# Grouped attention on one core: one store per head, V cast into place, loads in order of need, VectorE chains of eight

## The chip, the cores and the metric

One Trainium2 chip, one of its cores. The metric is the device time of one execution in microseconds (us), from repeated executions. A profile of one execution gives every instruction with start and duration. The span of a profile is some 1.8 us shorter than the time of the same execution. Engines: PE is TensorE, PEld its weight loads, DVE is VectorE, ACT is ScalarE, POOL is GpSimd, SP is SyncE. "L427" is line 427 of the kernel that was profiled, so the same line of code has other numbers in other kernels.

## The reference

Eight batches, eight query heads, two K/V heads (four query heads share one), 1024 positions, head size 64, all fp32:

```python
scores = scale * np.matmul(q_group, k_group.transpose(0, 1, 3, 2))
attn = np.exp(scores - np.max(scores, axis=-1, keepdims=True))
attn = attn / (np.sum(attn, axis=-1, keepdims=True) + 1e-08)
output[:, q_start:q_end] = np.matmul(attn, v_group)
```

## The kernel before

The work is cut into 128 jobs (a job is one half of the queries of one head) of eight cells (128 keys x 512 queries). A cell is one score matmul into PSUM (the memory that its matmuls write; the kernel has two buffers of it for each use, below called banks), an exponential, and four output matmuls, whose 65th column sums the weights. Two engines compute exponentials: ScalarE takes pairs of cells with its own function, VectorE takes single cells and computes the bits of a bf16 exponential, then corrects them in a chain of four steps over `GROUP` cells at once.

```python
GROUP = 4
...
def exp_bits(cell, n, g, slot):          # first step, cell by cell, out of PSUM
    nc.vector.tensor_scalar(out=groups[g][:, slot], in0=psum.pop(cell),
        scalar1=bits_scale, scalar2=bits_bias, op0=ALU.mult, op1=ALU.add)
def exp_curve(g, m, step):               # the chain, over m cells
    step 0: z = pd & 0x7F                # tensor_scalar
    step 1: y = z * A/128 + B            # tensor_scalar
    step 2: y = z * y                    # tensor_tensor
    step 3: pd = pd + y                  # tensor_tensor
...
def normalise(s):                        # job done: divide, then store half a head
    nc.vector.reciprocal(out=rec, in_=o[:, :, D])
    nc.vector.tensor_tensor(out=ost, in0=o[:, :, 0:D], in1=rec..., op=ALU.mult)
    nc.sync.dma_start(out=out[b, h]...[side], in_=ost)
```

(The chain is abridged to a line per step.) `make_plan` simulates the engines with fixed costs when the kernel is built, and lays down the order of all instructions. A cell goes to whichever of the two engines has a free PSUM bank first, in the order of the cells. Q, K and V are cast to bf16 by GpSimd's DMA into a scratch tensor in memory, Q and K come back through transposing DMAs, V through two placements.

The softmax here doesn't subtract the row's maximum and nothing guards it: scores larger than these inputs give would overflow.

Of the kernel before, what the change touches and what calls it, by code (L numbers as in the profile page):

```python
# [14 lines left out]
GROUP = 4  # L15


def make_plan(nj, nkc):
# [6 lines left out]
    QK, PV, EXP, P1, NORM = 0.214, 0.143, 0.925, 0.605, 0.57  # L25
    CHAIN = (0.73, 0.73, 1.26, 1.26)
    FROM_PE, FROM_ACT, FROM_DVE = 0.28, 0.18, 0.12
    LIVE_A, LIVE_D, PENDING, ONLY_A = 26, 6, 8, 14
    INF = 1e9
    n = nj * nkc  # L30
# [3 lines left out]
    nxt = 0  # L34
# [7 lines left out]

    def first_free(slots):
        return min(range(len(slots)), key=lambda s: slots[s])

    while normed < nj:
        best = None
        if nxt < n:
            ta = td = INF
            if open_a is not None:  # L50
                ta = max(pe, open_a["t"])
            elif live["A"] < LIVE_A:
                ta = max(pe, min(a_free))
            if pending < PENDING and nxt < n - ONLY_A and (cur or live["D"] < LIVE_D):
                td = max(pe, min(bank))
            t, to_d = (ta, 0) if ta <= td else (td, 1)
            if t < INF:
                best = min(best or (INF,), (t, 1 + to_d, "qk", to_d))
        for i, s in enumerate(open_jobs):
            for c in rem[s]:  # L60
                at = max(pe, ready.get(s * nkc + c, INF))
                if at < INF:
                    best = min(best or (INF,), (at, 3 + i, "pv", (s, c)))
        if len(open_jobs) < 2 and next_job < nj:
            at = max(pe, min(obank_free), min(ready.get(next_job * nkc + c, INF) for c in range(nkc)))
            if at < INF:
                best = min(best or (INF,), (at, 3 + len(open_jobs), "open", next_job))
        for q, p, kind in ((normq, 0, "norm"), (p1q, 1, "p1"), (chainq, 2, "chain")):
            if q:
                best = min(best or (INF,), (max(dve, q[0][0]), p, kind, 0))  # L70
        if cur and nxt >= n - ONLY_A and not p1q:
            best = min(best or (INF,), (dve, 9, "flush", 0))
        t, _, kind, arg = best
        if kind == "qk":
            cell = nxt
            nxt += 1
            pe = t + QK
            if not arg:
                if open_a is None:
                    slot = first_free(a_free)  # L80
                    a_id += 1
                    live["A"] += 1
                    open_a = {"slot": slot, "t": a_free[slot], "cells": []}
                    a_free[slot] = INF
                o = open_a
                ops.append((t, "qk", cell, "A", a_id, o["slot"], len(o["cells"])))
                o["cells"].append(cell)
                home[cell] = ("A", a_id)
                if len(o["cells"]) == 2 or nxt >= n:
                    act = max(act, pe + FROM_PE)  # L90
                    ops.append((act, "exp", a_id, tuple(o["cells"])))
                    act += EXP * len(o["cells"]) / 2
                    a_free[o["slot"]] = act + FROM_ACT
                    uses[("A", a_id)] = len(o["cells"])
                    for x in o["cells"]:
                        ready[x] = act + FROM_ACT
                    open_a = None
            else:
                k = first_free(bank)
                bank[k] = INF  # L100
                pending += 1
                ops.append((t, "qk", cell, "D", k, 0, 0))
                p1q.append((pe + FROM_PE, cell, k))
# [41 lines left out]
        elif kind == "flush":  # L145
            chainq.append((dve, d_id, cur, 0))
            cur = []
        else:
            _, g, cells, step = chainq.pop(0)
            ops.append((t, "chain", g, len(cells), step))  # L150
            dve = t + CHAIN[step] * len(cells) / GROUP
            if step + 1 < len(CHAIN):
                chainq.insert(0, (dve, g, cells, step + 1))
            else:
                pending -= len(cells)
                uses[("D", g)] = len(cells)
                for x in cells:
                    ready[x] = dve + FROM_DVE
# [4 lines left out]
def kernel(  # L163
# [27 lines left out]
    PIECE = 256  # L191
    scale = 1.0 / math.sqrt(D)
# [15 lines left out]
    qT_pool = ctx.enter_context(tc.tile_pool(name="qTpool", bufs=8))  # L208
    kT_pool = ctx.enter_context(tc.tile_pool(name="kTpool", bufs=4))
    pa_pool = ctx.enter_context(tc.tile_pool(name="papool", bufs=26))  # L210
    pd_pool = ctx.enter_context(tc.tile_pool(name="pdpool", bufs=6))
    tmp_pool = ctx.enter_context(tc.tile_pool(name="tmppool", bufs=2))
    ostage_pool = ctx.enter_context(tc.tile_pool(name="ostage", bufs=10))
# [11 lines left out]

    ident = const_pool.tile([128, 128], BF16)
    make_identity(nc, ident)
    vsets, ksets = [], []
    for s in range(2):
# [4 lines left out]
        for side in range(2):  # L234
            if s == 0:
                nc.vector.memset(ks[(1 - side) * D : (2 - side) * D, :, side, :], 0.0)
        ksets.append(ks)

# [41 lines left out]
    def place_v(b, g):  # L280
        for two in range(2):
            nc.sync.dma_start(
                out=vsets[b % 2][:, g, two * NHC : (two + 1) * NHC, 0:D],
                in_=scratch[("v", b, g)].rearrange(
                    "(c p two d) -> two p c d", p=128, two=2, d=D
                )[two],
            )

    def first_loads():

        staged = []
        for eng, src in ((nc.sync, k[0, 0]), (nc.scalar, q[0, 0])):
            f = first_pool.tile([128, NHC, 2, D], FP32, name=f"f{len(staged)}")
            eng.dma_start(
                out=f, in_=src.rearrange("(c p two) d -> p c two d", p=128, two=2)
            )
            staged.append(f)
        vf = first_pool.tile([128, NHC, 2, D], FP32, name="vf")
        nc.sync.dma_start(
            out=vf, in_=v[0, 0].rearrange("(c p two) d -> p c two d", p=128, two=2)  # L300
        )
        cast(("q", 0, 1), q[0, 1])
        for two in range(2):
            nc.gpsimd.tensor_copy(
                out=vsets[0][:, 0, two * NHC : (two + 1) * NHC, 0:D],
                in_=vf[:, :, two, :],
            )
        for side in range(2):
            nc.gpsimd.memset(ksets[1][(1 - side) * D : (2 - side) * D, :, side, :], 0.0)  # L309
        fk, fq = staged  # L310

        hk = first_pool.tile([128, NHC, 3, D], BF16, name="hk")
        nc.vector.tensor_copy(out=hk[:, :, 0:2, :], in_=fk)  # L313
        nc.vector.tensor_copy(out=hk[:, :, 2, :], in_=fk[:, :, 0, :])
        hq = first_pool.tile([128, NHC, 2 * D], BF16, name="hq")
        nc.scalar.copy(out=hq, in_=fq.rearrange("p c two d -> p c (two d)"))
        tk = dbanks[0].tile([128, 2, HALF], BF16, name="dps0")
        tq = dbanks[1].tile([128, HALF], BF16, name="dps1")
        for w in range(2):
            for c in range(NHC):  # L320
# [5 lines left out]
        for c in range(NHC):  # L326
            nc.tensor.transpose(tq[:, c * 128 : (c + 1) * 128], hq[:, c, :], ident)
        qT[(0, 0)] = qT_pool.tile([128, HALF], BF16, name="qT")
        lo, hi = slice(0, D), slice(D, 2 * D)
        nc.vector.tensor_copy(out=ksets[0][lo, 0, 0, 0:HALF], in_=tk[lo, 0, :])  # L330
        nc.scalar.copy(out=qT[(0, 0)], in_=tq)
        nc.vector.tensor_copy(out=ksets[0][lo, 0, 0, HALF:S], in_=tk[lo, 1, :])
        nc.vector.tensor_copy(out=ksets[0][hi, 0, 1, 0:HALF], in_=tk[hi, 1, :])
        nc.vector.tensor_copy(out=ksets[0][hi, 0, 1, HALF:S], in_=tk[hi, 0, :])
# [4 lines left out]
    temps = {}  # L339
    ops_of = {}  # L340
# [82 lines left out]
    def normalise(s):  # L423
# [4 lines left out]
        ost = ostage_pool.tile([128, NQS, D], FP32, name="ost")  # L428
        nc.vector.tensor_tensor(  # L429
            out=ost,  # L430
# [3 lines left out]
        )  # L434
        nc.sync.dma_start(
            out=out[b, h].rearrange("(s p two) d -> two p s d", p=128, two=2)[side],
            in_=ost,
        )


    events = []

    def at(t, f, *args):
        events.append((t, len(events), f, args))
# [4 lines left out]
    for op in plan:  # L449
        if op[1] == "qk":  # L450
            first_use.setdefault(op[2] // NKC, op[0])
        at(op[0], run[op[1]], *op[2:])
    for b in range(B):
        for h in range(H):
            if b == 0 and h == 0:
                continue
            th = first_use[(b * H + h) * 2]
            if (b, h) != (0, 1):
                at(th - 28.0, cast, ("q", b, h), q[b, h])
            for n in range(HALF // PIECE):  # L460
                at(th - 17.0 + n, transpose_q, b, h, n)
            if h % HPG == 0:
                g = h // HPG
                at(th - 38.0, cast, ("k", b, g), k[b, g])
                at(th - 33.0, cast, ("v", b, g), v[b, g])
                for n in range(HALF // PIECE):
                    at(th - 27.0 + n, transpose_k, b, g, n)
                for side in range(2):
                    for parity in range(2):
                        at(th - 20.0, place_k, b, g, side, parity)  # L470
                at(th - 15.0, place_v, b, g)
# [34 lines left out]
```

## Time and profile before

| | us |
|---|---|
| time, median (4 runs) | 397.54 (397.33 to 398.27) |
| span of the profile | 395.6 |
| start of the first exponential on ScalarE | 8.16 |
| first exponential to the end of the last | 380.05 |
| from there to the end of the span (the tail) | 7.4 |

These three stretches are how the run is read below. In the middle ScalarE is hardly ever idle, so the middle can shrink only if it has fewer exponentials or none of them waits; start and tail are chains of single steps. The lines of this profile are in the prediction.

### The profile page before, as it was taken

To read this page: it belongs to the slowest core of one execution; us is meant where nothing else is said; L and a number is where in the kernel's file an instruction comes from. 1 tells how busy PE (TensorE), PEld (TensorE's weight loads), DVE (VectorE), ACT (ScalarE), POOL (GpSimd) and SP (SyncE) were. 2 spreads that over 40 slices of the span, in tenths; PEclk is the share of its full clock that TensorE was granted. 3 is DMA by queue.
4 is the path that set the end of the run, shared out by engine and by line. 5 is a ranking of instruction groups with operands and counts; after the bars stand their busy time and mean duration, and the time that the engine had idled before them with its cause. 6 is when DMAs were issued, how large, how long until landed. Compare 5 with 4: busy or idle time off the path is not lost.

```text
span 395.6 us, 12683 instructions
## 1 busy us (share of the span) xinstructions
PE 365.7 (92%) x5043; PEld 233.0 (59%) x5132; DVE 375.8 (95%) x664; ACT 381.5 (96%) x415; POOL 86.6 (22%) x165
## 2 busy tenths in 40 slices
PE   4899999999999999999999999999999999999986
PEld 2455566565656556655656565565655666565655
DVE  4999999999999999999999999999999999999995
ACT  4999999999999999999999999999999999999992
POOL 5340303132041313113131040312214131120000
PEclk9999999999999999999999999999999999999999
DMA  4665866749676786847758686785965867574314
GB/s 106 106 125 111 163 107 127 128 86 160 103 139 130 132 143 101 142 90 145 115 103 141 111 141 112 118 143 98 155 109 115 149 132 121 99 130 99 68 28 94
DMA packets 134890, 46.72 MB, mean 118 GB/s; under 512 B 130848, under 2 KB 132384, under 8 KB 133344
## 3 DMA queue, kind: packets, MB, share of 16 engines
q1 hardware_dynamic: 129408, 29.52, 38.3%
q0 software_dynamic: 4896, 16.13, 27.0%
q8 instruction: 40, 0.66, 0.8%
q10 hardware_dynamic: 528, 0.26, 0.2%
q14 instruction: 18, 0.15, 0.2%
HBM read 27.13 MB, written 28.97 MB: 142 GB/s over the span
## 4 chain that ended last, share of the span: by engine, by line
ACT 67%; DVE 11%; PE 10%; issue 6%; DMA 3%; POOL 1%; SPq 0%
ACT pa L362 67%; PE ops L414 5%; PE aps L351 5%; DVE pd L371 3%; DVE y L402 2%; DVE pd L406 2%; DVE ost L429 1%; DMA vf<-in_v_dram 1%; PE dps L351 1%; DVE y L392 1%; DMA qT<-scr_q 1%; POOL kset L309 1%; DVE z L386 1%; DVE rec L427 1%; DMA scr_q<-in_q_dram 1%
## 5 line engine op out<-in xcount | busy, mean ns | idle before, releaser
L362 ACT ACTIVATE pa<-aps 128x1024 bf16<-128x1024 f32 x412 | 379.0, 1064 | 2.1 <-PE aps L351 1.3
L351 PE MATMUL aps<-qT,kset 128*128 128x512 bf16 x735 | 226.2, 379 | 15.5 <-ACT pa L362 13.6
L414 PEld LDWEIGHTS <-pa 128*128 128x128 bf16 x3296 | 134.5, 97 | 57.6 <-DVE ost L429 0.8
L414 PE MATMUL ops<-vset,pa 128*128 128x65 bf16 x3296 | 143.9, 193 | 3.4
L371 DVE TENSOR_SCALAR pd<-dps 128x512 uint16<-128x512 f32 x200 | 129.8, 682 | 2.2 <-PE dps L351 2.2
L351 PEld LDWEIGHTS <-kset 128*128 128x128 bf16 x1024 | 85.3, 97 | 66.3 <-issue 30.9
L248 POOL DMA_DIRECT2D scr_q<-in_q_dram x63 | 34.0, 540 | 173.4 <-PE aps L351 150.6
L351 PE MATMUL dps<-qT,kset 128*128 128x512 bf16 x200 | 64.5, 380 | 1.0
L406 DVE TENSOR_TENSOR pd<-pd,y 128x2048 uint16<-128x2048 uint16 x50 | 61.2, 1225 | 1.7
L402 DVE TENSOR_TENSOR y<-z,y 128x2048 f16<-128x2048 uint16 x50 | 61.2, 1225 | 1.7
L429 DVE TENSOR_TENSOR ost<-ops,rec 128x256 f32<-128x256 f32 x128 | 54.3, 425 | 4.4
L414 PEld LDWEIGHTS <-pd 128*128 128x128 bf16 x800 | 38.5, 97 | 29.8 <-DVE pd L406 7.9
L268 POOL DMA_DIRECT2D kset<-kT x60 | 32.2, 545 | 76.7 <-DMA kT<-scr_k 68.7
L414 PE MATMUL ops<-vset,pd 128*128 128x65 bf16 x800 | 45.3, 194 | 1.2
L392 DVE TENSOR_SCALAR y<-z 128x2048 f16<-128x2048 uint16 x50 | 34.3, 687 | 0.6
L386 DVE TENSOR_SCALAR z<-pd 128x2048 uint16<-128x2048 uint16 x50 | 34.2, 684 | 0.0
L427 DVE RECIPROCAL rec<-ops 128x4 f32<-128x4 f32 x128 | 22.6, 176 | 2.4 <-PE ops L414 1.9
L248 POOL DMA_DIRECT2D scr_v<-in_v_dram x15 | 7.6, 505 | 8.2 <-PE aps L351 7.1
L248 POOL DMA_DIRECT2D scr_k<-in_k_dram x15 | 8.1, 542 | 4.7 <-PE aps L351 4.3
L321 PE MATMUL dps<-ident,hk 128*128 128x128 bf16 x8 | 1.0, 311 | 5.0 <-DVE hk L313 5.0
L321 PEld LDWEIGHTS <-hk 128*128 128x128 bf16 x8 | 0.8, 141 | 5.0 <-DVE hk L313 5.0
L309 POOL MEMSET kset<- 64x2048 bf16 x2 | 3.6, 1798 | 0.1
(20 smaller groups left out, 9.7 us busy)
## 6 DMA issues: line engine op xcount, KB each, us to landing
out_dram<-ost SPq DMA_DIRECT2D x128, 128.0 KB, 3.2
scr_q<-in_q_dram POOLq DMA_DIRECT2D x63, 128.0 KB, 3.5
kset<-kT POOLq DMA_DIRECT2D x60, 64.0 KB, 2.7
qT<-scr_q SPq DMA_TRANSPOSE x126, 3.6
scr_k<-in_k_dram POOLq DMA_DIRECT2D x15, 128.0 KB, 4.2
scr_v<-in_v_dram POOLq DMA_DIRECT2D x15, 128.0 KB, 3.9
vset<-scr_v SPq DMA_DIRECT2D x30, 64.0 KB, 3.8
kT<-scr_k SPq DMA_TRANSPOSE x30, 3.4
```

The lines of the kernel that those rows point to most:

```text
L248: dma = nc.gpsimd.dma_start(out=scr.rearrange("(p f) -> p f", f=1024), in_=src.rearrange("(p s) d -> p (s d)", s=1024 // D),)
L268: nc.gpsimd.dma_start(out=ksets[b % 2][side * D : (side + 1) * D, g, side, parity * HALF : (parity + 1) * HALF], in_=kT[(b, g)][parity * D ...
L351: last_score[0] = nc.tensor.matmul(dst, lhsT=ksets[b % 2][:, h // HPG, side, c * 128 : (c + 1) * 128], rhs=qT[(b, h)], start=True, stop=Tr ...
L362: nc.scalar.activation(out=pt[:, 0:m], in_=psum.pop(("A", n))[:, 0:m], func=AF.Exp, scale=scale)
L371: nc.vector.tensor_scalar(out=groups[g][:, slot], in0=psum.pop(cell), scalar1=bits_scale, scalar2=bits_bias, op0=ALU.mult, op1=ALU.add,)
L386: nc.vector.tensor_scalar(out=z, in0=pd, scalar1=0x7F, scalar2=None, op0=ALU.bitwise_and)
L392: nc.vector.tensor_scalar(out=y, in0=temps[g][0], scalar1=CURVE_A / 128.0, scalar2=CURVE_B, op0=ALU.mult, op1=ALU.add,)
L402: nc.vector.tensor_tensor(out=y, in0=z, in1=y, op=ALU.mult)
L406: nc.vector.tensor_tensor(out=pd, in0=pd, in1=y, op=ALU.add)
L414: nc.tensor.matmul(ops_of[s][:, qs, :], lhsT=p_of[cell][:, qs * 128 : (qs + 1) * 128], rhs=vsets[b % 2][:, h // HPG, c, :], start=opens an ...
L427: nc.vector.reciprocal(out=rec, in_=o[:, :, D])
L429: nc.vector.tensor_tensor(out=ost, in0=o[:, :, 0:D], in1=rec.unsqueeze(2).to_broadcast([128, NQS, D]), op=ALU.mult,)
```

## The change

Four things at once. **Chains of eight**: half as many chain instructions, each twice as long. **Jobs further on**: ScalarE works through the jobs in order, while VectorE takes at most two cells a job, from jobs up to six or seven ahead, so that its long chains are finished when a job needs them. **Loads in order of need**: the first K and Q come in halves, the array is warmed by dummy matmuls, V follows, other loads are spread over time. **V and stores**: V is cast by one DMA straight into its place, and a head's two halves are stored together. Pool sizes and the plan's other constants changed with these, and the zeroing of the second K buffer went from GpSimd to DMA copies.

```diff
-GROUP = 4
+GROUP = 8
...
-    QK, PV, EXP, P1, NORM = 0.214, 0.143, 0.925, 0.605, 0.57
-    CHAIN = (0.73, 0.73, 1.26, 1.26)
+    EXP, AND, LINE, PRODUCT = (0.065, 0.4265), (0.20, 0.133), (0.20, 0.133), (0.16, 0.27)
+    CHAIN = (AND, LINE, PRODUCT, PRODUCT)        # fixed part, part per cell
+    LIVE_A, LIVE_D, PENDING, PER_JOB, LEAD, RAMP, AHEAD, FIRST_PV = 28, 5, 16, 2, 6, 3, 0.08, 2.0
...
+        lead = min(LEAD, job_a // RAMP)
+        job_d = max(job_d, job_a + lead)
...
-    def place_v(b, g):                            # two reads of a cast scratch copy
+    def place_v(b, g, two):
+        nc.gpsimd.dma_start(
+            out=vsets[b % 2][:, g, two * NHC : (two + 1) * NHC, 0:D],
+            in_=v[b, g].rearrange("(c p two) d -> two p c d", p=128, two=2)[two])
...
+        last_score[0] = keep_warm(WARM)           # WARM = 26 dummy matmuls
+        for n, half in enumerate(halves):         # K and Q by halves
+            nc.scalar.copy(out=hk[:, half, 0:2, :], in_=fk[:, half])
...
+            if op[2] >= len(jobs) - 2:            # the last head by halves
+                at(op[0] + 0.01, put_out, b, h, slice(side, side + 1))
+            elif side:                            # the others whole, a little later
+                at(op[0] + 1.5, put_out, b, h, slice(0, 2))
```

(Cut to its core; some calls are joined on a line.)

## The prediction

> **What bounds the kernel now.** I read the page first (busy shares and slices), then a table of stretches, the waits, the timeline of VectorE in mid-run, and the timelines of the first 10 and the last 20 us.
>
> The page's shares and slices:
> ```profile
> PE 365.7 (92%) x5043; PEld 233.0 (59%) x5132; DVE 375.8 (95%) x664; ACT 381.5 (96%) x415; POOL 86.6 (22%) x165
> PE   4899999999999999999999999999999999999986
> DVE  4999999999999999999999999999999999999995
> ACT  4999999999999999999999999999999999999992
> ```
> Three engines look full at once; only the first slice and the last two are thin. The table of stretches (duration; then busy us and instruction count of PE, weight loads, VectorE, ScalarE, GpSimd; clock; DMA share; GB/s) separates them:
> ```profile
> 50.00:350.00 300.00, 285.69 (x3981) 183.13 (x4052) 292.53 (x519) 299.42 (x327) 67.85 (x127) 1.00 0.71 123
> 390.00:396.00 6.00, 1.81 (x59) 1.68 (x55) 1.70 (x6) 0.00 (x0) 0.00 (x0) 0.92 0.46 95
> ```
> ScalarE is busy 299.4 of 300 us, VectorE 292.5. The list of waits gives ScalarE's exponentials only 1.3 us of waiting for scores in the whole run, and the scores 13.6 us of waiting for an exponential to free its bank. So in the middle the bound is **ScalarE at its own rate, with VectorE beside it taking the share of the cells it can**: a balance of two engines. TensorE is not the bound: warm scores start 0.21 us apart (a pair spans 0.59 where one lasts 0.38) and a cell's four output matmuls take 0.13 (80 in 2.63 at the end), so 1024 cells need about 1024 x 0.34 = 350 us; its 286 of 300 includes modelled tails.
>
> The costs, from the groups (busy us, mean ns):
> ```profile
> L362 ACT ACTIVATE pa<-aps 128x1024 bf16<-128x1024 f32 x412 | 379.0, 1064 | 2.1 <-PE aps L351 1.3
> L371 DVE TENSOR_SCALAR pd<-dps 128x512 uint16<-128x512 f32 x200 | 129.8, 682 | 2.2 <-PE dps L351 2.2
> ```
> 412 exponentials of two cells are 824 cells, VectorE has 200. One exponential every 0.917 us (364.1 busy us over 397 in the stretch from 15 to 380), although one lasts 1.064: neighbours overlap. Likewise VectorE must be costed by starts, not by means. Its timeline (start, duration):
> ```profile
> 211.46 0.69 DVE L386 TENSOR_SCALAR z<-pd 128x2048 uint16<-128x2048 uint16 x1
> 212.06 0.18 DVE L427 RECIPROCAL rec<-ops 128x4 f32<-128x4 f32 x1
> 212.27 0.42 DVE L429 TENSOR_TENSOR ost<-ops,rec 128x256 f32<-128x256 f32 x1
> 212.61 0.68 DVE L392 TENSOR_SCALAR y<-z 128x2048 f16<-128x2048 uint16 x1
> 213.33 1.22 DVE L402 TENSOR_TENSOR y<-z,y 128x2048 f16<-128x2048 uint16 x1
> 214.59 1.22 DVE L406 TENSOR_TENSOR pd<-pd,y 128x2048 uint16<-128x2048 uint16 x1
> 215.73 1.28 DVE L371 TENSOR_SCALAR pd<-dps 128x512 uint16<-128x512 f32 x2
> 216.93 0.69 DVE L386 TENSOR_SCALAR z<-pd 128x2048 uint16<-128x2048 uint16 x1
> ```
> Start to start: AND 0.60 (an unrelated instruction follows), line 0.72, product 1.26 (their consumers follow), last step 1.14: a chain of four is **3.72 us**. First step (1.28 for two, next start 1.20 later) 0.60, a normalisation 0.21 + 0.34 = 0.55. Check: 200 x 0.60 + 50 x 3.72 + 128 x 0.55 = 376.4, beside 378.6 us from VectorE's first cell (9.44) to the end of its last chain (388.08). The costing closes within 1%.
>
> The two ends, from the timeline:
> ```profile
> 4.49 0.43 DVE L313 CAST hk<-f 128x512 bf16<-128x512 f32 x1 [1.40 <-DMA f<-in_k_dram]
> 5.81 0.63 PE L327 MATMUL dps<-ident,hq 128*128 128x128 bf16 x4
> 6.48 0.58 ACT L331 COPY qT<-dps 128x512 bf16<-128x512 bf16 x1 [0.93 <-PE dps L327]
> 7.11 1.86 PE L351 MATMUL aps<-qT,kset 128*128 128x512 bf16 x4 [0.67 <-ACT qT L331]
> 8.16 8.83 ACT L362 ACTIVATE pa<-aps 128x1024 bf16<-128x1024 f32 x9 [1.10 <-PE aps L351]
> ...
> 375.21 13.00 ACT L362 ACTIVATE pa<-aps 128x1024 bf16<-128x1024 f32 x14
> 386.85 1.23 DVE L406 TENSOR_TENSOR pd<-pd,y 128x2048 uint16<-128x2048 uint16 x1
> 389.18 2.63 PE L414 MATMUL ops<-vset,pa 128*128 128x65 bf16 x80
> 392.06 0.42 DVE L429 TENSOR_TENSOR ost<-ops,rec 128x256 f32<-128x256 f32 x1
> ```
> The span of 395.6 is therefore **8.16 us before the first exponential, 380.05 us of exponentials (to 388.21), 7.4 us of tail**. The tail is long because the last VectorE chain ends at 388.08, at the same moment as the last exponential, and jobs already computed queue behind its cells: 96 output matmuls remain.
>
> **What the Trainium skill says.** (1) "VectorE: DVE Perf Modes", Side-by-side: where the cycles go, gives 693 ns for a four-per-cycle and 1224 ns for a two-per-cycle instruction of 2048 elements; the trace has 684 to 687 and 1225. By its The TRN2 errata section a large tile pays the per-instruction cost once. By that page 2048 elements stream in 2048/4/0.96 GHz = 0.533 us or 2048/2/0.96 = 1.067, which leaves 0.07 to 0.19 us a step fixed. (2) "TensorE: Matmul & The Clock Gate", Part 1, has an idle array at half clock until about 3.4 us of activity. The trace agrees: the first four scores come about 0.43 us apart, later pairs 0.21, though the page's clock row shows no throttling. (3) "SBUF — State Buffer", SBUF: two separate sides, says that GpSimd cannot write descriptors while VectorE runs a two-port instruction. Here the longest of 63 cast issues on GpSimd is 716 ns beside a median of 521: little harm before.
>
> **The change, part by part.**
> Chains of eight: by the streams above the steps become 1.13, 1.25, 2.33 and 2.21 us, 6.92 for eight cells instead of 7.44, so a cell costs 0.60 + 0.865 = 1.465 instead of 1.53. That frees about 13 us of VectorE in 200 cells, but not 13 us of time: cells move to VectorE until both end together. Before: VectorE 1.53 D + 72.4 (normalising and waits), ScalarE (1024 - D) x 0.459 + 1.9 (waits) = 471.9 - 0.459 D; equal at D = 200.8 and 379.7 us (measured 200 and 380.05). After: 1.465 D + 72.4 = 471.9 - 0.459 D gives D = 207.6 and 376.6 us: **-3.1 us**.
> Cells from jobs further on: the plan takes at most two per job, up to seven jobs ahead, so VectorE gets no new cell while ScalarE does the last six jobs: 6 x (8 - 1.6) = 38 cells, 17.5 us. I estimate 9 us of chains begun and 4 us of normalising in that time, so about 4.5 us of VectorE idle: 3.1 cells, shared out at 1/0.459 + 1/1.465 = 2.86 cells per us, **+1.1 us**. In exchange nothing waits for a chain at the end: after the last exponential come its 0.17, two cells of output (0.26), the array's 0.26, 0.6 of normalising and the last store (392.48 to 395.6, 3.1): 4.4 instead of 7.4, **-3.0 us**.
> Start: K and Q come first and in halves, V after them. The DMA is 67% busy in the first 5 us, so I take 0.3 us off the landing (4.2 to 4.4). TensorE warmed by 26 dummy matmuls does its last transposes in some 0.6 instead of 1.5 us. The first two scores are 0.4 us quicker warm. First exponential at about 6.55: **-1.6 us**.
> Stores: 64 of 256 KB with 512-byte runs instead of 128 of 128 KB. They hide behind compute except the last one, which stays a half: 0. V straight: 15 casts to memory and 30 reads fall away, 32 placements by GpSimd come; GpSimd is 22% busy and the loads lead their use by over 8 us: 0.
> Sum: -3.1 + 1.1 - 3.0 - 1.6 = -6.6, so 397.45 - 6.6 = **390.8 us** (-1.7%).
>
> **Rivals.** (a) Ends and middle both give all they can: start at 5.8, 376.2, tail 4.0, plus 1.8 between span and time: 387.8, -2.4%. For it: the plan's constants are close to the costs that I read, so it is tuned. Against it: each term must be at its floor. (b) Loads late in the ramp: the chain of waits before runs in its first 19 us through casts and transposes (GpSimd's two memsets held casts back until 10.37). These memsets go, but V placements of 512 short runs come into the same GpSimd queue; if one head is late, ScalarE stalls 2 to 4 us: 393 to 395. (c) VectorE's chain steps are twice as long; the steps on two ports hold the port 1.1 to 1.3 us at a time, and the two score banks wait through a 2.3 us product. If TensorE, in order, blocks behind such a score, ScalarE starves: with 26 groups at 0.3 us, +8 us: 398. Against it: ScalarE waited 0.2 us in the middle before, and a product of 1.26 was there already. (d) All of VectorE's saving counts in full (-13 us): 381. Against it is the balance: ScalarE alone still needs 408 x 0.917 us.
>
> **Range and chances.** The floor of (a) sets the low side, (b) the high side: 388.0 to 394.0. The line for faster by 2% is 389.5, which needs most terms to come out better than mine: 0.35. Slower by 2% (405.4) needs (c) several times over: 0.02. Within 2%: 0.63.
>
> **What would show it.** Right: about 408 exponentials, some 208 VectorE cells in 26 chains, steps of 4096 elements near 1.1 to 1.3 and 2.2 to 2.3 us start to start, first exponential at 6.3 to 6.8, 375 to 379 us of exponentials, and 4 to 5 us from the last one's end to the span's end. Wrong: exponentials waiting for scores by over 3 us in the middle (c), TensorE waiting for a transposed head in the first 30 us (b), or a first exponential later than 7.2.

## The result and the profile after

The changed kernel took **393.19 us** (median of 4, 393.12 to 395.51; a fifth execution took 392.97) beside 397.54 (397.33 to 398.27). The ratio was 0.9897, with a 95% interval of 0.9863 to 0.9932: 1.0% faster, and by the 2% measure the same. A ratio here is the mean time of one kernel's fast runs over that of the other's of the same rounds, so it is not quite the ratio of the medians.

The execution that was profiled was the slow one of these, 395.5 us; why, the experiments show. So the profile after is that of an ordinary execution, a later run of the unedited kernel with a span of 391.1. From its page, the busy shares and the two exponential groups (columns as before: busy us and mean ns, then idle time before):

```profile
PE 363.0 (93%) x5077; PEld 233.0 (60%) x5166; DVE 366.2 (94%) x573; ACT 380.4 (97%) x416; POOL 106.9 (27%) x184
...
L427 ACT ACTIVATE pa<-aps 128x1024 bf16<-128x1024 f32 x411 | 377.7, 1065 | 1.7 <-PE aps L416 1.7
...
L436 DVE TENSOR_SCALAR pd<-dps 128x512 uint16<-128x512 f32 x202 | 130.9, 682 | 2.1 <-PE dps L416 1.5
```

The table of stretches, the same 300 us of the middle:

```profile
50.00:350.00 300.00, 284.77 (x4063) 183.66 (x4135) 291.22 (x451) 300.00 (x328) 82.08 (x135) 1.00 0.69 120
```

ScalarE is busy in all of the 300 us, as before, and VectorE in 291.2 instead of 292.5. But ScalarE still has 411 exponentials of the 412 it had, and VectorE has taken 202 cells instead of 200. The timeline of VectorE in mid-run (start, duration):

```profile
211.34 1.22 DVE L457 TENSOR_SCALAR y<-z 128x4096 f16<-128x4096 uint16 x1
212.47 0.18 DVE L492 RECIPROCAL rec<-ops 128x4 f32<-128x4 f32 x1
...
214.80 2.28 DVE L467 TENSOR_TENSOR y<-z,y 128x4096 f16<-128x4096 uint16 x1
217.11 2.29 DVE L471 TENSOR_TENSOR pd<-pd,y 128x4096 uint16<-128x4096 uint16 x1
219.32 1.28 DVE L436 TENSOR_SCALAR pd<-dps 128x512 uint16<-128x512 f32 x2
```

Start to start the line step took 1.13 us (an unrelated step follows), the products 2.31 and 2.21. The same product of the chain before this one started at 200.10, so VectorE repeats itself every 14.70 us, the time of 16 exponentials: 8 of its cells to 32 of ScalarE.

The two ends, from the timeline:

```profile
5.66 0.65 ACT L389 COPY qT<-dps 128x256 bf16<-128x256 bf16 x2 [0.95 <-PE dps L383]
...
6.36 0.81 PE L416 MATMUL aps<-qT,kset 128*128 128x512 bf16 x3 [0.62 <-ACT qT L389]
...
6.99 1.94 ACT L427 ACTIVATE pa<-aps 128x1024 bf16<-128x1024 f32 x2 [0.68 <-PE aps L416]
...
8.70 0.61 PE L416 MATMUL dps<-qT,kset 128*128 128x512 bf16 x2 [1.31 <-DVE kset L350]
...
9.78 1.02 ACT L427 ACTIVATE pa<-aps 128x1024 bf16<-128x1024 f32 x1 [0.85 <-PE aps L416]
```

```profile
379.13 6.58 ACT L427 ACTIVATE pa<-aps 128x1024 bf16<-128x1024 f32 x7
...
385.61 0.90 PE L479 MATMUL ops<-vset,pa 128*128 128x65 bf16 x24
...
386.77 0.42 DVE L495 TENSOR_TENSOR ost<-ops,rec 128x256 f32<-128x256 f32 x1
```

The first exponential starts at 6.99, the last ends at 385.71, the last normalisation at 387.19 and the span at 391.1. By stretches:

| us | before | predicted | after, ordinary execution |
|---|---|---|---|
| start to the first exponential | 8.16 | 6.55 | 6.99 |
| exponentials | 380.05 | 378.05 (-3.1 + 1.1) | 378.7 |
| tail | 7.4 | 4.4 | 5.4 |
| span | 395.6 | 389.0 | 391.1 |

All three stretches shrank, and each by less than predicted: by 0.4, 0.7 and 1.0 us. The experiments look for these three remainders (0.4 + 0.7 + 1.0 = 2.1, as the spans have it), and for what each part of the change is worth.

### The profile page after: what moved, and what is told of

It is laid out like the page before. It is cut to its first block, busy times and chain, and to the rows that moved or that the text cites. A ratio compares the mean times of both kernels' runs of the same rounds, so it can differ in the third digit from the quotient of the medians.

```text
span 393.7 us, 12506 instructions
## 1 busy us (share of the span) xinstructions
PE 371.0 (94%) x5166; PEld 234.3 (60%) x5166; DVE 366.2 (93%) x573; ACT 380.7 (97%) x416; POOL 107.1 (27%) x184
## 4 chain that ended last, share of the span: by engine, by line
ACT 81%; PE 11%; issue 6%; DMA 1%; DVE 0%
ACT pa L427 80%; PE aps L416 5%; PE ops L479 4%; PE dps L416 2%; DMA fk<-in_k_dram 1%; DVE kset L350 0%; PE dps L341 0%; ACT qT L389 0%; PE ops L368 0%; PE dps L383 0%; DVE ost L495 0%; ACT hk L376 0%; DVE rec L492 0%
## 5 line engine op out<-in xcount | busy, mean ns | idle before, releaser
L416 PE MATMUL aps<-qT,kset 128*128 128x512 bf16 x822 | 245.8, 380 | 15.8 <-ACT pa L427 13.8
L479 PE MATMUL ops<-vset,pa 128*128 128x65 bf16 x3288 | 149.1, 194 | 0.0
L416 PE MATMUL dps<-qT,kset 128*128 128x512 bf16 x202 | 71.4, 383 | 1.2 <-DVE kset L350 0.9
L471 DVE TENSOR_TENSOR pd<-pd,y 128x4096 uint16<-128x4096 uint16 (+1 forms) x26 | 57.8, 2224 | 0.3
L467 DVE TENSOR_TENSOR y<-z,y 128x4096 f16<-128x4096 uint16 (+1 forms) x26 | 57.7, 2220 | 0.1
L479 PE MATMUL ops<-vset,pd 128*128 128x65 bf16 x808 | 41.3, 193 | 0.0
L457 DVE TENSOR_SCALAR y<-z 128x4096 f16<-128x4096 uint16 (+1 forms) x26 | 31.5, 1210 | 0.0
L451 DVE TENSOR_SCALAR z<-pd 128x4096 uint16<-128x4096 uint16 (+1 forms) x26 | 31.3, 1202 | 0.0
L319 POOL DMA_DIRECT2D vset<-in_v_dram x32 | 26.4, 831 | 2.1 <-issue 1.9
L368 PE MATMUL ops<-blank 128*128 128x128 bf16 x34 | 4.6, 312 | 1.0 <-DVE blank L258 1.0
```

What stands on the lines that cost most here:

```text
L319: nc.gpsimd.dma_start(out=vsets[b % 2][:, g, two * NHC : (two + 1) * NHC, 0:D], in_=v[b, g].rearrange("(c p two) d -> two p c d", p=128, t ...
L416: last_score[0] = nc.tensor.matmul(dst, lhsT=ksets[b % 2][:, h // HPG, side, c * 128 : (c + 1) * 128], rhs=qT[(b, h)], start=True, stop=Tr ...
L451: nc.vector.tensor_scalar(out=z, in0=pd, scalar1=0x7F, scalar2=None, op0=ALU.bitwise_and)
L457: nc.vector.tensor_scalar(out=y, in0=temps[g][0], scalar1=CURVE_A / 128.0, scalar2=CURVE_B, op0=ALU.mult, op1=ALU.add,)
L467: nc.vector.tensor_tensor(out=y, in0=z, in1=y, op=ALU.mult)
L471: nc.vector.tensor_tensor(out=pd, in0=pd, in1=y, op=ALU.add)
```

## The experiments

Twelve runs in three calls; kernels of a call shared a chip and the runs of the kernel before. The third call was on another chip than the first, the second on a third one. All results were correct. Medians of before: 397.69, 397.84 and 397.43. The unedited changed kernel was not run in the second call, so c1 to c4 are held against its 392.95 from the two other chips.

### The changed kernel again: a1_again and d0_again

No edit.

> The changed kernel again, unedited, to get a profile of an ordinary execution: the profiled one took 395.5 us where four others took 393.0 to 393.2. Theory (clock): the extra 2.4 us is TensorE running at half rate until 13.5 us (scores 0.43 us apart), a matter of when the array's clock opens, so it shows only in the first 15 us: an ordinary execution has its first exponential near 7.1 us, no waits of ScalarE for scores after it, and the same 5.4 us tail; time 393.2. Rival (profiling): a profiled execution always shows the slow ramp, and the profile is again of 395.5.

> The changed kernel once more, on the chip that runs the three below, as their measure and to count how often the array's clock opens late: 392.9 in most executions, some at 395.5. Theory [...]: about one in five late. Rival (a chip's own habit): all or none.

Measured: 392.96 (392.87 to 393.00) and 392.95 (392.79 to 393.18), ratios 0.9880 and 0.9889, so an ordinary execution is of **392.95 us**, and "a profiled execution always shows the slow ramp" has fallen: these profiles are of ordinary executions. In the slow execution of 395.5 the timeline of PE and ACT shows the difference:

```profile
6.48 1.44 PE L416 MATMUL aps<-qT,kset 128*128 128x512 bf16 x3 [0.52 <-ACT qT L389]
...
7.53 1.02 ACT L427 ACTIVATE pa<-aps 128x1024 bf16<-128x1024 f32 x1 [1.10 <-PE aps L416]
...
11.58 1.02 ACT L427 ACTIVATE pa<-aps 128x1024 bf16<-128x1024 f32 x1 [1.75 <-PE aps L416]
...
13.83 0.59 PE L416 MATMUL aps<-qT,kset 128*128 128x512 bf16 x2
```

Three scores span 1.44 us there and 0.81 in the ordinary execution; a pair spans 0.59 only from 13.83 on. The array ran at half rate until then, the first exponential came 0.5 us later, and the exponentials took 380.8 us instead of 378.7: together the 2.6 us between the spans (393.7 and 391.1); the tail is the same. (The list of waits has ScalarE waiting 3.8 us for scores instead of 1.7; the wait before the first exponential, 1.10 and 0.68, is part of these sums, here and below.) So the clock theory holds for this execution, a *late clock* from here on; its forecast that no waits would follow in an ordinary execution does not: 0.85 and 0.16 us remain. How often: of 37 executions of this kernel and of the six variants below that keep its start (a2, a3, c1 to c4), five took 2 us or more above the lowest of their kernel. Four of these fell among the 16 of the second chip, none among the 16 of the two others, so a chip's habit is not excluded, though "all or none" is not what that chip shows. Only one of the five has a profile, so that the other four were late clocks too is not shown; d2_all below has a slow execution of another kind.

### Without the dummy matmuls: a4_no_warm

```diff
-    WARM = 26
+    WARM = 1
...
-            keep_warm(2)          # both calls in the loop
```

> 33 of the 34 dummy matmuls of the start left out. Theory (clock): without them the array stays at half rate until some 3.4 us of real work are done, so every execution looks like the slow profiled one or worse: 395.5 to 396. Rival: the dummy matmuls are worth nothing, since the array went slow again in spite of them: 393.2.

Measured: 396.03, 395.34 and 394.94, and one execution of 742.54 us, which was the profiled one. The median of the three ordinary ones is 2.4 us above 392.95 (they are 2.0 to 3.1 above it), near the clock theory's 395.5 to 396, and the rival's 393.2 falls: the dummies are worth about that. That the three ran at half rate for longer is argued, since none of them has a profile. (The 3.4 us is the Trainium skill's figure that the prediction names; two other profiles without dummies, of the kernel before and of e1_old_start, show full rate 4.5 and 3.7 us after their first transpose.) The fourth was not expected by anyone. Its timeline in mid-run:

```profile
301.42 0.71 PE L414 MATMUL dps<-qT,kset 128*128 128x512 bf16 x1
301.85 1.17 PE L414 MATMUL aps<-qT,kset 128*128 128x512 bf16 x2
```

One score starts 0.43 after the other, at 300 us into the run. In the stretch from 50 to 700 us PE was busy 625 of 650 us and ScalarE 371: the array stayed at half rate for the whole execution and became the bound, while the record of the granted clock read 1.000. No other execution did so, with or without dummies; one case can't tell whether the missing dummies caused it.

### Chains of four: a2_group4

```diff
-GROUP = 8
+GROUP = 4
-    ... = 28, 5, 16, 2, 6, 3, 0.08, 2.0
+    ... = 28, 10, 16, 2, 6, 3, 0.08, 2.0
-    pd_pool ... bufs=5
+    pd_pool ... bufs=10
```

> Chains of four instead of eight, all else as in the changed kernel (as many cells pending, buffers of the same total size). Theory (balance): a cell costs VectorE 1.53 instead of 1.465 us, so the plan gives it 196 cells instead of 202 and ScalarE 414 exponentials instead of 411, 3 x 0.917 = 2.8 us more: 396.0. Rival (the chain's saving was lost, since the change brought only 412 to 411 exponentials): chains of four are as good, 393 to 394.

Measured: **398.7** (397.73 to 399.30), ratio 1.0022 to before: 5.7 us slower than chains of eight, twice what the balance said. Its group of exponentials and the end of its last chain:

```profile
L427 ACT ACTIVATE pa<-aps 128x1024 bf16<-128x1024 f32 x414 | 380.3, 1069 | 3.0 <-PE aps L416 3.0
```

```profile
379.49 10.19 ACT L427 ACTIVATE pa<-aps 128x1024 bf16<-128x1024 f32 x11
...
390.06 1.22 DVE L471 TENSOR_TENSOR pd<-pd,y 128x2048 uint16<-128x2048 uint16 x1
```

The three exponentials more are there (3 x 0.917 = 2.8 us). Beside them ScalarE waited 3.0 us for scores instead of 1.7, which is 1.3 more, and the last chain ended at 391.28, after the last exponential (389.68), so the tail is 6.7 instead of 5.4. 2.8 + 1.3 + 1.3 = 5.4, and the spans differ by 5.3. So the saving of the chain of eight was not lost, and the second expectation falls. But the 5.7 us are not all the chain's. The 1.3 us of waits are one wait, ScalarE's at 29.88 (1.26 us), for a K that its DMA placed late:

```profile
28.80 0.61 PE L416 MATMUL dps<-qT,kset 128*128 128x512 bf16 x2 [1.59 <-DMA kset<-kT]
```

And the plan takes a chain of four to be dearer than it is: 3.94 us (0.72 + 4 x 0.806 in its constants) where the prediction read 3.72. `make_plan` alone, called without a chip, repeats the counts of the runs (414 exponentials here, 411 in the changed kernel); with the measured costs of c3 below it gives fours 412 and eights 410. So 5.7 us is more than eights would bring to a plan made for fours.

### VectorE's cells from near jobs: a3_no_lead

```diff
-    ... = 28, 5, 16, 2, 6, 3, 0.08, 2.0
+    ... = 28, 5, 16, 2, 0, 3, 0.08, 2.0      # LEAD = 0
```

> VectorE's cells from the job that ScalarE is at or the next, instead of six to seven jobs on; chains of eight kept. Theory: a chain of eight needs some 14 us from its first score to its last step, longer than the 6 us in which ScalarE does two jobs, so output matmuls wait for chains, the 28 buffers of finished exponentials fill, ScalarE stalls, and the end waits for a last chain: 405 to 430. Rival (buffers absorb it): the lead matters only at the end, 394 to 397.

Measured: **424.6** (424.36 to 424.63), ratio 1.0674. The list of waits names what the first theory named:

```profile
PEld L479 <- DVE pd L471: 16.7, 11, 3.7
ACT pa L427 <- PE dps L416: 16.0, 7, 2.3
```

Output matmuls waited 16.7 us for the ends of chains, and ScalarE 16.0 us in seven waits of 2.29 us; before the one that ended at 346.16, for instance, TensorE had stood until 343.47 before an output matmul that needed a chain. Whether the 28 buffers were full the trace doesn't say. Chains of eight need cells from jobs further on; the two parts of the change are one. The plan had even given VectorE more here, 224 cells, and ScalarE only 400 exponentials; the time went into waits (ScalarE 21.9 us in all) and into a tail of 24 us, from 398.91 to 422.9.

### V through memory: c1_old_v

```diff
+            nc.sync.dma_start(out=dst, in_=scratch[("v", b, g)]...)   # all but the first V
...
+                casts.append((th - 13.5 - 20.0 * spare, ("v", b, g), v[b, g]))
```

> V through memory again (a cast to a scratch tensor on GpSimd's queue, then two placements from SyncE's queue), all else as in the changed kernel. Theory (hidden anyway): V is needed 8 us or more after it lands, ScalarE's waits in the middle stay at 0, time 393.0 within 0.5. Rival (it was worth something: 15 casts and 30 reads fewer leave the queues free for Q and K): 394 to 396, with waits of scores for a transposed head in the first 40 us.

Measured: 393.28, 392.84, 395.65 and 395.23. The first two are ordinary executions, equal to 392.95; the profile (of 393.28) has ScalarE waiting 2.2 us instead of 1.7 and a tail of 5.0; TensorE has no wait for a head of Q in its list, and one of 0.5 us for a placement of K. The other two look like late clocks but have no profile. So V's new way is worth nothing that two runs can show; that it changes how often an execution is slow is neither shown nor excluded.

### The stores: c2_half_stores and c4_last_store

c2 stores every half head right after its normalisation, as the kernel before did; c4 only takes the delay off the last whole-head store.

```diff
 c2:
-            if op[2] >= len(jobs) - 2: ...
-            elif side: at(op[0] + 1.5, put_out, b, h, slice(0, 2))
+            at(op[0] + 0.01, put_out, b, h, slice(side, side + 1))
 c4:
-                at(op[0] + 1.5, put_out, b, h, slice(0, 2))
+                at(op[0] + (0.01 if op[2] >= len(jobs) - 4 else 1.5), put_out, b, h, slice(0, 2))
```

> One store per half head, issued right after its normalisation, as before, 128 stores of 256-byte runs. Theory (hidden, but for the end): no change in the middle; the last three stores of the changed kernel are issued back to back because one is held back 1.5 us, so half stores without the hold bring the tail from 5.4 to about 4.7 us: 392.3. Rival (the larger runs free DMA time that matters): 393.5 to 395.

> The store of the last but one head issued at once instead of 1.5 us later, nothing else. Theory (the tail is 5.4 instead of the predicted 4.4 us, of which 0.8 is the last store queueing behind the two before it): tail 4.6, time 392.2. Rival (the last store's 3.9 us is what a store of 256-byte runs takes here): 393.0.

Measured: c2 391.96 (391.75 to 394.57), c4 392.41 (392.30 to 392.65). By the profiles the first two stretches are those of the changed kernel (first exponentials at 6.87 and 6.96, last ones ending at 385.72 and 385.69), and the tails are 4.4 and 4.8 instead of 5.4. The timelines of SyncE's issues in the last 7 us, first of the changed kernel, then of c4:

```profile
386.24 1.50 SPq L504 DMA_DIRECT2D out_dram<-ost  x3
```

```profile
384.81 2.77 SPq L504 DMA_DIRECT2D out_dram<-ost  x3
```

In the changed kernel three stores of 512 KB in all are issued in one run of 1.50 us, and the last of them lands 3.9 us after its data is ready (387.19 to 391.1); before, that took 3.1 (392.48 to 395.6), in c4 3.3 and in c2 2.9. With the first of the three sent 1.4 us earlier the tail shrinks by 0.6, with everything in halves by 1.0. So both theories of the tail hold, and both rivals fall: the larger runs free nothing that matters, and the 3.9 us is not what such a store takes by itself.

### The plan's costs: c3_true_costs

```diff
-    ..., AND, LINE, PRODUCT = ..., (0.20, 0.133), (0.20, 0.133), (0.16, 0.27)
-    CHAIN = (AND, LINE, PRODUCT, PRODUCT)
+    ..., AND, LINE, PRODUCT = ..., (0.07, 0.133), (0.19, 0.133), (0.19, 0.267)
+    CHAIN = (AND, LINE, PRODUCT, (0.07, 0.267))
```

> Only the plan's constants of VectorE's chain steps changed to the starts measured in the trace (AND 0.07 + 0.133 a cell, line 0.19 + 0.133, products 0.19 and 0.07 + 0.267: 6.9 instead of 7.2 us for eight). Theory (the plan leaves VectorE work it could do, because it takes a chain to be dearer than it is): the plan gives it 205 cells and ScalarE 410 exponentials, 391.5 to 392.3. Rival (VectorE is full in the middle, 14.47 of each 14.69 us; more cells only make TensorE wait for its banks): 393 to 394.5.

Measured: **391.61** (390.95 to 393.69), ratio 0.9854. The profile has VectorE with 205 cells and ScalarE with 410 exponentials; they take from 7.02 to 384.61, 377.6 us instead of 378.7, and the tail is 4.6. The rival falls: VectorE had room. Three of the four times lie below the lowest of the changed kernel's eight (392.79). But the cells account for only 1.1 us of the 1.9 between the two profiles. The other 0.8 is the tail: the new plan happens to spread the last three stores, whose code is unedited, over 2.99 us instead of 1.50, as c4 does on purpose.

```profile
L427 ACT ACTIVATE pa<-aps 128x1024 bf16<-128x1024 f32 x410 | 376.4, 1065 | 1.8 <-PE aps L416 1.7
```

```profile
383.26 2.99 SPq L504 DMA_DIRECT2D out_dram<-ost  x3
```

### The start: e1_old_start and d1_start

e1 puts the whole `first_loads` of the kernel before into the changed kernel (without its memsets of the second K buffer, which the changed kernel does elsewhere). d1 keeps the new start and edits it:

```diff
+        put_q(first)                # first half of Q copied before the second half's transposes
         turn_k(0, then)
         turn_q(then)
+        put_q(then)
+        put_k(0, 0, first)
+        put_k(0, 0, then)
+        turn_k(1, every)            # was done between the first scores
+        keep_warm(3)
+        for side, parity in ((0, 1), (1, 0), (1, 1)):
+            put_k(side, parity, every)
```

> The start of the kernel before (whole loads of K, Q and V at once, V cast by GpSimd, no dummy matmuls, all five copies in one go) in the changed kernel. Theory (the start is worth the 1.2 us by which the first exponential came earlier, since ScalarE's waits after it are about equal in both): first exponential at 8.2, 394.1. Rival (the loads' order helps the whole ramp): ScalarE waits for heads in the first 40 us too, 395.5 or more.

> Only the start edited: the two halves of Q copied as they come, the second transposes of K done before the first scores instead of between them, two dummy matmuls moved into the wait before the first score. Theory (the start fell short of the predicted 1.6 us because the Q copies waited for the last transpose and the bank of VectorE's first score was freed only at 8.65): first exponential near 6.4 instead of 7.0 and no wait of 0.85 us after the second exponential, 391.7; and late clocks rarer, since the array has no hole of 0.6 us before its first score. Rival (what binds the start is the landing of the second halves at 4.3 and 4.8): 392.5 to 393.

Measured: e1 395.3 (394.53 to 395.88), which is 2.35 us more than the changed kernel. Its first exponential is at 8.27, 1.3 later, the exponentials take 380.5 us instead of 378.7, and the tail is 4.9 instead of 5.4; by these the profiles differ by 2.6. One wait is of TensorE for a K that a DMA places (1.28 us, until 29.19); the new start has 0.3 us of it there, and the kernel before has none. So in the changed kernel the new start is worth about twice what the first exponential alone shows, and the first theory, 394.1, falls for its rival (395.5 or more), nearly.

d1: 393.1 (392.94 to 393.17), nothing gained. In its timeline:

```profile
7.02 8.55 ACT L443 ACTIVATE pa<-aps 128x1024 bf16<-128x1024 f32 x9 [1.01 <-PE aps L432]
...
15.03 0.59 PE L432 MATMUL dps<-qT,kset 128*128 128x512 bf16 x2 [0.65 <-DMA qT<-scr_q]
```

The wait of 0.85 us after the second exponential is gone: nine exponentials run without a gap. But the scores then reach a head of Q that has not landed, and ScalarE waits 0.52 at 16.09. And the first exponential is no earlier (7.02): the second half of Q was copied by 6.00 instead of 6.31, but the transposes of K and the dummies that now stand before the scores kept TensorE until 6.39. The ramp is bound by the next thing as soon as one is taken away. Neither expectation named these two. None of the four executions was slow, too few to say whether late clocks became rarer.

### All edits together: d2_all

The start of d1, the costs of c3, and half stores at once for the last two heads.

> That start, the measured chain costs in the plan, and half stores without the hold for the last two heads, together. Theory (the three act at different ends of the run and add): 393.0 - 1.2 - 1.4 - 0.9 = 389.5, against the kernel before -2.0%. Rival (they overlap): 390.5 to 391.

Measured: **390.62** (390.07 to 392.34, six runs), ratio 0.9825 (0.9812 to 0.9839) to before. It beats both kernels, by 6.8 and 2.3 us, and is still the same as the kernel before by the 2% measure. The theory's sum was wrong in two places: d1 brought nothing of its 1.2, and the tail was counted twice, since c3's 1.4 held 0.8 of it (d2's tail is 4.5, c3's 4.6). Without both the sum is 391.5, so 0.9 us are not accounted for; part of that may be the chip (before took 397.84 beside c3 and 397.43 here). Its only profile is of the slowest execution, 2.3 us above the lowest, and that was no late clock: TensorE had its full rate from 4.45 on, but waited 1.65 us for a transposed head of Q, until 12.16, and 1.16 for a placed K, until 29.12. So the loads of the first heads are what is left of the ramp.

## Why the prediction was right or wrong

The time lay in the range (388.0 to 394.0) and in the likeliest class. The point, 390.8, was 2.15 us below an ordinary execution (392.95), and the steps account for it. All three stretches missed to the same side. The range held because its high side was set for rival (b), which did not come; that is luck.

**What bounds the middle: right.** ScalarE was busy in 300.0 of 300 us, at 0.919 us an exponential (14.70 / 16). The middle followed the number of exponentials, in c3 too: one fewer than the changed kernel and 1.1 us less.

**The chain's costs: right; how far they turn into cells: mis-sized.** The measured starts of 1.13, 2.31 and 2.21 are within 0.02 us of those predicted for the same kind of follower (estimates, from the page's rates and the chain before). The term that failed is "equal at D = 207.6", less the 3.1 cells of the end: 204.5 cells, and VectorE got 202. The balance of the real costs was not what decided; the plan decided, with a chain of 7.2 us for eight cells (0.20 x 2 + 0.16 x 2 + 8 x 0.806 in its constants) where the trace has 6.9. It settled on 8 cells in 40, 20.0%, where my balance has 207.6 / 1024 = 20.3%. c3, with the real costs in the plan, had 205 cells, as the balance had it. The constants stood in the diff, to be compared with the trace; I wrote in a rival that they were close, and left it there.

**The end of VectorE's work: right.** Its last first step ended at 367.56, 18.2 us before the last exponential (17.5 predicted), and in these it was busy 14.1 us, so idle 4.1 (4.5 predicted).

**The tail: the mechanism right, two terms off.** No chain is waited for any more, but 4.4 became 5.4. The store takes 0.8 of that: I took the last store's 3.1 us from before and called the new stores "0", and did not see that holding a whole head's store back by 1.5 us puts three stores into the last moments. c2 and c4 show that, and c3 by chance. The remaining 0.2 is output matmuls still queued at the last exponential: 0.84 to the last reciprocal (385.71 to 386.55) where I had 0.69.

**The start: mis-sized in three terms.** The first exponential came at 6.99, not 6.55. Q's second half landed at 4.80, where before all of it had landed at 4.93: 0.13 us won, not the 0.3 that I took off. From there to the end of the last transpose took 0.83 us where I had 0.6, because the array was still at half rate for most of them (0.42 us for two, until 5.3). The two copies of Q took 0.65 instead of 0.58. Only the scores' 0.4 came as predicted. What followed was not in my sum: ScalarE's listed waits after its first exponential grew from 0.2 us to 1.0. That e1 shows the new start to be worth 2.35 us does not make up for my 1.6: part of it is the K that the old start places late under the new plan, a wait that the kernel before did not have.

**V: zero, as predicted,** within what two ordinary executions can show. **The stores: not zero, but a loss** of 0.6 to 1.0 us at the end, and no gain elsewhere.

**The rivals.** (a) did not come; the plan's constants were not tuned to the trace. (b), a late head, did not strike the changed kernel (a weight load waited 0.3 us for a K placed by 27.28, and ScalarE did not feel it), but a late head or K appeared in a2, d1, d2 and e1. (c), a score that waits for VectorE's bank behind long steps and blocks TensorE, did not come either: such waits were 0.2 us in the ordinary execution and 1.8 even in a3. The block that a3 shows is another, output matmuls that wait for unfinished chains; no rival named it, and the lead holds it off. (d) was excluded, as argued. What no rival had is the late clock: 2.4 us in one of the five executions of the first measurement.

## What to carry to other kernels

Where two engines share the same work, what one of them saves moves the time only by the shift of the balance, and a fixed plan shifts it only as far as its own constants say (here 1.1 us were left by a chain costed at 7.2 instead of 6.9); compare them with the trace before anything else. When two edits are measured one by one, see by stretches what each moved before adding them. A longer chain needs work from further ahead, and its price is paid at the end of the run, where the last store deserves to be sent alone and at once. And when a start is shortened, look at once for the load that comes next.

## What the Trainium skill lacked or had wrong

- "TensorE: Matmul & The Clock Gate", Part 1: it has the array opened by some 3.4 us of sustained activity, and calls the ramp's share under 1%. Here the first dummy ran at 0.99 us, and full rate was seen from 4.1 us on in a3_no_lead, 4.45 in d2_all, 5.46 in a1_again and between 5.6 and 6.4 in d0_again, 3.1 to 5.4 us later, which roughly agrees; in one execution it came only at 13.83, and that cost 2.4 us of 393 (0.6%), so the share agrees too. Its caveats tell of a throttle seen stuck at a quarter of the clock for 50 us and more; here the array stayed at half rate (scores 0.43 us apart) for a whole execution of 742 us, with the granted clock recorded as 1.000.
- "VectorE: DVE Perf Modes", The TRN2 errata: its 58 cycles plus the stream is said to under-predict a single instruction's duration. That is so (1.22 us lasts a step of 4096 elements), but it is what the trace shows from start to start where an unrelated instruction follows: 1.13 us, where an estimate from the page's rates is 4096/4/0.96 GHz = 1.07 and 58 cycles = 0.06. Where the consumer follows, the product's start is 2.31 us before the next, with 2.13 of stream by the same estimate. No page gives times for the two cases side by side.
- No page says what several stores issued one behind another cost at the end of a kernel: three of them in 1.50 us made the last one land 3.9 us after its data was ready, instead of 3.1 before, 3.3 with the first of them sent 1.4 us earlier (c4) and 2.9 with halves (c2).
